# Row sums on one core: fifteen rows per partition in two buffers, in place of eight in five

## The chip, the cores and the metric

One core of a Trainium2 chip runs the kernel. The metric is the device time of one execution in microseconds (us); the time of a kernel is the median of its runs. The engines that matter here are VectorE (DVE in the profile), ScalarE (ACT), SyncE (SP), which issues the loads, and the core's 16 DMA engines, which carry them. A queue of an engine, written SPq or ACTq, holds its DMA issues in program order.

## What is computed

```python
def setup_inputs():
    batch, seq, dim = 32, 512, 1024
    return {
        "x": np.random.randn(batch, seq, dim).astype(np.float32),
        "divisor": float(dim),
    }

def reference(x, divisor):
    return (np.sum(x, axis=-1) / divisor).astype(np.float32)
```

The input is 16,384 rows of 1024 floats, 4 KiB a row and 67.1 MB in all. The output is one float per row, 64 KB.

## The kernel before

The rows are spread over the 128 partitions of the on-chip memory, 128 rows to a partition. What is loaded is summed along its rows by two engines side by side: DVE reduces several rows of a piece with one instruction (`reduce_sum`, L58), and ACT sums one row per instruction by copying it into a scratch tile `junk` with a running sum (`act_sum`, L53; the profile shows it as an ACTIVATE and a read of the accumulator). The function `sums` divides a piece: the last `for_act` rows go to ACT, the others to DVE.

The bulk is 15 tiles (the loop over `g`). A tile is 1024 consecutive rows, a block of 4 MiB, in which partition p has the 8 rows from 8p on, a contiguous run of 32 KiB (`xr`). Each tile is one load on SP's queue (L64) into one of five buffers (`bufs=5`); DVE takes 5 of its rows and ACT 3. A load into a buffer waits on SP until both engines have read what was there before. After the 7th and the 15th tile DVE multiplies the sums so far by 1/divisor (L68), and ACT's queue issues their store (L69), in runs of 8 floats.

The last 1024 rows, `xt`, are again 8 rows per partition. They come in pieces that get smaller, each with memory of its own: 4, 2 and 1 rows (`tail`, loaded at L73, half of each piece, rounded up, to ACT), and the last row in a half and two quarters (`last`, L81). DVE sums the half (L82), ACT the first quarter, then DVE multiplies the 7 finished tail sums by 1/divisor (L84), sums the last quarter (L85), adds the three parts (L86) and multiplies (L87), and SP stores the 8 results of each partition (L88).

Every engine runs its instructions in program order. So the store L69 stands on ACT's queue ahead of the tail's sums, and the tail's loads stand on SP's queue behind the bulk's. The waits between engines are put in by the tile framework, from which tile each instruction reads and writes.

Of the kernel before, what the change touches and what calls it, by code (L numbers as in the profile page):

```python
# [1 line left out]

# [4 lines left out]

F32 = mybir.dt.float32
ADD = mybir.AluOpType.add
MULT = mybir.AluOpType.mult  # L10
COPY = mybir.ActivationFunctionType.Copy
AX = mybir.AxisListType.X


@with_exitstack
def kernel(
    ctx: ExitStack,
    tc: tile.TileContext,
    x: bass.AP,
    divisor: float,  # L20
    out: bass.AP,
):
    nc = tc.nc
    xf = x.flatten_outer_dims()
    N, D = xf.shape
    P = nc.NUM_PARTITIONS
    scale = 1.0 / float(divisor)
    J = N // P
    assert J * P == N

    R, T = 8, 8
    G = (J - T) // R
    assert G * R + T == J
    n0 = G * P * R
    xr = bass.AP(tensor=x.tensor, offset=0, ap=[[R * D, P], [P * R * D, G], [D, R], [1, D]])
    xt = bass.AP(tensor=x.tensor, offset=n0 * D, ap=[[T * D, P], [D, T], [1, D]])
    ob = bass.AP(tensor=out.tensor, offset=0, ap=[[R, P], [P * R, G], [1, R]])
    ot = bass.AP(tensor=out.tensor, offset=n0, ap=[[T, P], [1, T]])  # L40
    tail = [4, 2, 1]
    pool = ctx.enter_context(tc.tile_pool(name="bulk", bufs=5))
    one = ctx.enter_context(tc.tile_pool(name="one", bufs=1))
    psum = ctx.enter_context(tc.tile_pool(name="junk", bufs=1, space=bass.MemoryType.PSUM))

    res = one.tile([P, G, R], F32, name="res")
    rest = one.tile([P, T], F32, name="rest")
    part = one.tile([P, 4], F32, name="part")
    junk = psum.tile([P, D], F32, name="junk")

    def act_sum(dst, src):
        n = src.shape[-1]
        nc.scalar.activation(junk[:, :n], src, COPY, accum_out=dst)  # L53

    def sums(t, o, rows, for_act):
        d = rows - for_act
        if d:
            nc.vector.reduce_sum(out=o[:, :d], in_=t[:, :d, :], axis=AX)  # L58
        for r in range(d, rows):
            act_sum(o[:, r : r + 1], t[:, r, :])  # L60

    for g in range(G):
        t = pool.tile([P, R, D], F32, name="t")
        nc.sync.dma_start(out=t, in_=xr[:, g])  # L64
        sums(t, res[:, g], R, 3)
        if g in (G // 2 - 1, G - 1):
            a = 0 if g < G - 1 else G // 2
            nc.vector.tensor_scalar_mul(out=res[:, a : g + 1], in0=res[:, a : g + 1], scalar1=scale)  # L68
            nc.scalar.dma_start(out=ob[:, a : g + 1], in_=res[:, a : g + 1])  # L69
    j = 0  # L70
    for k, rows in enumerate(tail):
        t = one.tile([P, rows, D], F32, name=f"tail{k}")
        nc.sync.dma_start(out=t, in_=xt[:, j : j + rows, :])  # L73
        sums(t, rest[:, j : j + rows], rows, (rows + 1) // 2)
        j += rows


    h, q = D // 2, D // 4
    last = one.tile([P, D], F32, name="last")
    for a, b in ((0, h), (h, h + q), (h + q, D)):  # L80
        nc.sync.dma_start(out=last[:, a:b], in_=xt[:, j, a:b])  # L81
    nc.vector.reduce_sum(out=part[:, 0:1], in_=last[:, 0:h], axis=AX)  # L82
    act_sum(part[:, 1:2], last[:, h : h + q])
    nc.vector.tensor_scalar_mul(out=rest[:, :j], in0=rest[:, :j], scalar1=scale)  # L84
    nc.vector.reduce_sum(out=part[:, 2:3], in_=last[:, h + q : D], axis=AX)  # L85
    nc.vector.reduce_sum(out=part[:, 3:4], in_=part[:, 0:3], axis=AX)  # L86
    nc.vector.tensor_scalar_mul(out=rest[:, j : j + 1], in0=part[:, 3:4], scalar1=scale)  # L87
    nc.sync.dma_start(out=ot, in_=rest)  # L88


# [1 line left out]
_INS = ['x', 'divisor']  # L92
_OUTS = [((32, 512), 'float32')]

_NUMBERS = {'divisor': 1024.0}


# [26 lines left out]
```

## Time and profile before

| what | value |
|---|---|
| median of 3 runs | 165.42 us (165.16 to 165.44) |
| profiled execution, its own time | 165.44 us |
| its span, first to last instruction | 163.7 us |
| DVE busy | 87.5 us (53%) |
| ACT busy | 58.1 us (35%) |
| DVE idle, waiting for a bulk load | 72.3 us |
| ACT idle, waiting for a bulk load | 98.4 us |
| DMA queue q1, the loads, share of 16 engines | 95.8% |
| DMA queue q10, small packets | 1952 packets, 0.06 MB, 0.7% |
| median time from issue to landing, a bulk load of 4 MiB | 43.0 us |

Times in the trace count from the start of the span. A landing is the moment at which an engine that waited for a load is let go. The time from issue to landing has the loads queued ahead in it: five may be under way.

### The profile page before, as it was taken

Reading aid. Unit: us, or ns where it says so; the run is one execution under the profiler, and the core shown is the slowest. Engines: PE = TensorE matmul, PEld = TensorE weight load, DVE = VectorE, ACT = ScalarE, POOL = GpSimd, SP = SyncE. Lnnn points to the kernel's source line nnn. Section 1 sums busy time; section 2 is a strip of 40 time slices with the busy share of each in tenths; the row PEclk is TensorE's granted clock in tenths of the full one; section 3 lists DMA queues with packets and bytes.
Section 4 is the critical chain, followed back from the end, with each engine's and each line's share of the span. In section 5 each row is a group of like instructions: output and inputs, shape, how many; then the busy total and the mean of one; then the engine's idle time right before and its main releaser. Section 6 shows DMA issues by size and latency. Waiting matters only on the chain.

```text
span 163.7 us, 226 instructions
## 1 busy us (share of the span) xinstructions
DVE 87.5 (53%) x24; ACT 58.1 (35%) x101; POOL 0.2 (0%) x4
## 2 busy tenths in 40 slices
DVE  0008548092763909367291843909357291854991
ACT  3008043070613508052260803508052260804393
POOL 0000000000000000000000000000000000000000
DMA  7899999998999999989999999999999999998980
GB/s 256 384 424 473 392 481 408 408 489 384 440 456 392 481 408 408 489 384 424 473 393 457 433 395 481 401 417 481 393 425 465 401 449 433 401 481 372 416 268 1
DMA packets 5121, 67.18 MB, mean 410 GB/s; under 512 B 2432, under 2 KB 2688, under 8 KB 2944
## 3 DMA queue, kind: packets, MB, share of 16 engines
q1 hardware_dynamic: 3168, 67.11, 95.8%
q10 hardware_dynamic: 1952, 0.06, 0.7%
q14 instruction: 1, 0.01, 0.0%
HBM read 67.11 MB, written 0.07 MB: 410 GB/s over the span
## 4 chain that ended last, share of the span: by engine, by line
DMA 83%; DVE 11%; issue 2%; ACT 1%; SPq 1%; ACTq 0%; DVEq 0%
DMA t<-in_x_dram 83%; DVE res L58 10%; ACT junk L53 1%; SPq L64 1%; ACTq L69 0%; DVE part L85 0%; DVE res L68 0%; DVE rest L84 0%; DVE part L86 0%; DVE rest L87 0%; DVEq L86 0%; DVEq L68 0%
## 5 line engine op out<-in xcount | busy, mean ns | idle before, releaser
L58 DVE TENSOR_REDUCE res<-t 128x5 f32<-128x5120 f32 x15 | 82.3, 5488 | 72.3 <-DMA t<-in_x_dram 72.3
L53 ACT ACTIVATE junk<-t 128x1024 f32<-128x1024 f32 x45 | 46.2, 1027 | 99.3 <-DMA t<-in_x_dram 98.4
L53 ACT ACTIVATION_READ_ACCUMULATOR junk<-t 128x1 f32 x45 | 8.4, 186 | 0.0
L53 ACT ACTIVATE junk<-tail 128x1024 f32<-128x1024 f32 x4 | 4.1, 1027 | 2.8 <-DVE res L68 2.7
L58 DVE TENSOR_REDUCE rest<-tail 128x2 f32<-128x2048 f32 (+1 forms) x2 | 3.4, 1745 | 0.0
L53 ACT ACT_TABLE_LOAD x1 | 1.3, 1283 | 0.7 <-PEq L105 0.7
L82 DVE TENSOR_REDUCE part<-last 128x1 f32<-128x512 f32 x1 | 0.7, 686 | 0.2 <-DMA last<-in_x_dram 0.2
L53 ACT ACTIVATION_READ_ACCUMULATOR junk<-tail 128x1 f32 x4 | 0.7, 186 | 0.0
L84 DVE TENSOR_SCALAR rest<-rest 128x7 f32<-128x7 f32 x1 | 0.2, 170 | 0.9 <-ACT junk L53 0.9
L68 DVE TENSOR_SCALAR res<-res 128x56 f32<-128x56 f32 (+1 forms) x2 | 0.4, 193 | 0.2
L85 DVE TENSOR_REDUCE part<-last 128x1 f32<-128x256 f32 x1 | 0.4, 410 | 0.0
L53 ACT ACTIVATE junk<-last 128x256 f32<-128x256 f32 x1 | 0.4, 387 | 0.0
L86 DVE TENSOR_REDUCE part<-part 128x1 f32<-128x3 f32 x1 | 0.2, 156 | 0.1
L53 ACT ACTIVATION_READ_ACCUMULATOR junk<-last 128x1 f32 x1 | 0.2, 186 | 0.0
L87 DVE TENSOR_SCALAR rest<-part 128x1 f32<-128x1 f32 x1 | 0.2, 156 | 0.0
L105 POOL MEMSET const-bfloat16-1.0<- 128x1 bf16 x1 | 0.1, 102 | 0.0
L105 POOL MEMSET const-uint8-127<- 128x1 uint8 x1 | 0.1, 102 | 0.0
L105 POOL MEMSET const-float32-1.0<- 128x1 f32 x1 | 0.1, 99 | 0.0
L105 POOL MEMSET const-float32-0.0<- 128x1 f32 x1 | 0.1, 98 | 0.2 <-issue 0.2
## 6 DMA issues: line engine op xcount, KB each, us to landing
t<-in_x_dram SPq DMA_DIRECT2D x15, 4096.0 KB, 43.0
tail<-in_x_dram SPq DMA_DIRECT2D x1, 2048.0 KB, 11.0
tail<-in_x_dram SPq DMA_DIRECT2D x1, 1024.0 KB, 13.1
tail<-in_x_dram SPq DMA_DIRECT2D x1, 512.0 KB, 13.9
last<-in_x_dram SPq DMA_DIRECT2D x1, 256.0 KB, 14.1
last<-in_x_dram SPq DMA_DIRECT2D x2, 128.0 KB, 13.9
out_dram<-res ACTq DMA_DIRECT2D x1, 32.0 KB, 4.9
out_dram<-res ACTq DMA_DIRECT2D x1, 28.0 KB, 66.4
```

The costliest lines, as they stand in the source:

```text
L53: nc.scalar.activation(junk[:, :n], src, COPY, accum_out=dst)
L58: nc.vector.reduce_sum(out=o[:, :d], in_=t[:, :d, :], axis=AX)
L64: nc.sync.dma_start(out=t, in_=xr[:, g])
L68: nc.vector.tensor_scalar_mul(out=res[:, a : g + 1], in0=res[:, a : g + 1], scalar1=scale)
L82: nc.vector.reduce_sum(out=part[:, 0:1], in_=last[:, 0:h], axis=AX)
L84: nc.vector.tensor_scalar_mul(out=rest[:, :j], in0=rest[:, :j], scalar1=scale)
L85: nc.vector.reduce_sum(out=part[:, 2:3], in_=last[:, h + q : D], axis=AX)
L86: nc.vector.reduce_sum(out=part[:, 3:4], in_=part[:, 0:3], axis=AX)
L87: nc.vector.tensor_scalar_mul(out=rest[:, j : j + 1], in0=part[:, 3:4], scalar1=scale)
L105: nc = _bacc.Bacc("TRN2", target_bir_lowering=False, num_devices=1)
```

## The change

The rows are dealt out in another way: partition p now owns the 128 consecutive rows from 128p on, so that its share of the input is one contiguous run of 512 KiB, and its share of the output one run of 512 B. The bulk is 8 loads of 15 rows per partition (a run of 60 KiB in each) into two buffers; DVE takes 8 rows of a load and ACT 7. The tail has the same pieces as before (4, 2 and 1 rows, and a row in a half and two quarters), now from the end of each partition's own run. All sums go to one tile `res` of 128 columns. The multiplies and stores inside the bulk loop are gone: one multiply takes the first 127 columns at the end, and one store from SP writes everything.

```diff
-    R, T = 8, 8
-    G = (J - T) // R
-    assert G * R + T == J
-    n0 = G * P * R
-    xr = bass.AP(tensor=x.tensor, offset=0, ap=[[R * D, P], [P * R * D, G], [D, R], [1, D]])
-    xt = bass.AP(tensor=x.tensor, offset=n0 * D, ap=[[T * D, P], [D, T], [1, D]])
-    ob = bass.AP(tensor=out.tensor, offset=0, ap=[[R, P], [P * R, G], [1, R]])
-    ot = bass.AP(tensor=out.tensor, offset=n0, ap=[[T, P], [1, T]])
+    xr = x.tensor.reshape((P, J, D)).ap()
+    out_v = out.tensor.reshape((P, J)).ap()
+    bulk = [15] * 8
     tail = [4, 2, 1]
-    pool = ctx.enter_context(tc.tile_pool(name="bulk", bufs=5))
+    assert sum(bulk) + sum(tail) + 1 == J
+    pool = ctx.enter_context(tc.tile_pool(name="bulk", bufs=2))
...
-    res = one.tile([P, G, R], F32, name="res")
-    rest = one.tile([P, T], F32, name="rest")
+    res = one.tile([P, J], F32, name="res")
...
-    def sums(t, o, rows, for_act):
+    def sums(t, j, rows, for_act):
         d = rows - for_act
         if d:
-            nc.vector.reduce_sum(out=o[:, :d], in_=t[:, :d, :], axis=AX)
+            nc.vector.reduce_sum(out=res[:, j : j + d], in_=t[:, :d, :], axis=AX)
         for r in range(d, rows):
-            act_sum(o[:, r : r + 1], t[:, r, :])
+            act_sum(res[:, j + r : j + r + 1], t[:, r, :])
 
-    for g in range(G):
-        t = pool.tile([P, R, D], F32, name="t")
-        nc.sync.dma_start(out=t, in_=xr[:, g])
-        sums(t, res[:, g], R, 3)
-        if g in (G // 2 - 1, G - 1):
-            a = 0 if g < G - 1 else G // 2
-            nc.vector.tensor_scalar_mul(out=res[:, a : g + 1], in0=res[:, a : g + 1], scalar1=scale)
-            nc.scalar.dma_start(out=ob[:, a : g + 1], in_=res[:, a : g + 1])
     j = 0
+    for rows in bulk:
+        t = pool.tile([P, 15, D], F32, name="t")
+        nc.sync.dma_start(out=t[:, :rows, :], in_=xr[:, j : j + rows, :])
+        sums(t, j, rows, rows * 7 // 15)
+        j += rows
     for k, rows in enumerate(tail):
         t = one.tile([P, rows, D], F32, name=f"tail{k}")
-        nc.sync.dma_start(out=t, in_=xt[:, j : j + rows, :])
-        sums(t, rest[:, j : j + rows], rows, (rows + 1) // 2)
+        nc.sync.dma_start(out=t, in_=xr[:, j : j + rows, :])
+        sums(t, j, rows, (rows + 1) // 2)
         j += rows
...
-        nc.sync.dma_start(out=last[:, a:b], in_=xt[:, j, a:b])
+        nc.sync.dma_start(out=last[:, a:b], in_=xr[:, j, a:b])
...
-    nc.vector.tensor_scalar_mul(out=rest[:, :j], in0=rest[:, :j], scalar1=scale)
+    nc.vector.tensor_scalar_mul(out=res[:, :j], in0=res[:, :j], scalar1=scale)
...
-    nc.vector.tensor_scalar_mul(out=rest[:, j : j + 1], in0=part[:, 3:4], scalar1=scale)
-    nc.sync.dma_start(out=ot, in_=rest)
+    nc.vector.tensor_scalar_mul(out=res[:, j : j + 1], in0=part[:, 3:4], scalar1=scale)
+    nc.sync.dma_start(out=out_v, in_=res)
```

## The prediction

> **What bounds the kernel now.** I read the chain that ended last first, because it says which resource the end hangs on, and the memory line beside it.
>
> ```profile
> HBM read 67.11 MB, written 0.07 MB: 410 GB/s over the span
> ...
> DMA 83%; DVE 11%; issue 2%; ACT 1%; SPq 1%; ACTq 0%; DVEq 0%
> ```
>
> The span is a read stream of 67 MB, with little around it. So two things have a price: the pace of the stream, and what is left once the stream has delivered its last large piece. For the pace I cut the span at the landings of the bulk loads (columns: stretch, its length, DVE, ACT and POOL busy, clock, DMA share, GB/s).
>
> ```profile
> 22.60:32.30 9.70, 5.49 (x1) 3.45 (x6) 0.00 (x0) 1.00 1.00 432
> ...
> 90.70:100.90 10.20, 5.46 (x2) 3.45 (x6) 0.00 (x0) 1.00 1.02 435
> ```
>
> All 16 DMA engines are busy all the time, and DVE and ACT are half idle. The timeline has DVE starting on the second load at 22.62 and on the eighth at 80.89 us: (80.89 - 22.62) / 6 = 9.712 us per load of 8 rows per partition, 1.214 us a row. One interval took 10.22 us, and the DMA view of that window shows what only it has, one packet of instructions:
>
> ```profile
> q1 hardware_dynamic: 151, 4.42, 99.7%
> q10 hardware_dynamic: 151, 0.00, 0.8%
> q14 instruction: 1, 0.01, 0.2%
> ```
>
> While q10, the small packets of the first result store, runs (its DMA is on its way from 77.0 to 143.4 us), the other intervals are hardly longer: 110.61 to 139.77 is 3 x 9.720.
>
> Then the end, in the timeline (start, length, engine and line):
>
> ```profile
> 149.47 5.49 DVE L58 TENSOR_REDUCE res<-t 128x5 f32<-128x5120 f32 x1 [4.21 <-DMA t<-in_x_dram]
> ...
> 155.29 0.38 ACTq L69 DMA_DIRECT2D out_dram<-res  x1
> 155.72 1.03 ACT L53 ACTIVATE junk<-tail 128x1024 f32<-128x1024 f32 x1 [2.68 <-DVE res L68]
> ...
> 156.90 1.03 ACT L53 ACTIVATE junk<-tail 128x1024 f32<-128x1024 f32 x1
> ...
> 159.26 1.03 ACT L53 ACTIVATE junk<-tail 128x1024 f32<-128x1024 f32 x1
> 160.22 0.19 ACT L53 ACTIVATION_READ_ACCUMULATOR junk<-tail 128x1 f32 x1
> 160.44 0.39 ACT L53 ACTIVATE junk<-last 128x256 f32<-128x256 f32 x1
> 160.44 0.17 DVE L84 TENSOR_SCALAR rest<-rest 128x7 f32<-128x7 f32 x1 [0.94 <-ACT junk L53]
> ...
> 161.22 0.16 DVE L87 TENSOR_SCALAR rest<-part 128x1 f32<-128x1 f32 x1
> 161.44 0.35 SPq L88 DMA_DIRECT2D out_dram<-rest  x1
> ```
>
> Call T the landing of the last bulk load, 149.44 in the chain. The last arithmetic ends at 161.38 = T + 11.94, and ACT sets it: it is through with its 3 bulk rows at 153.04, stands 2.68 us behind the store L69 in its own queue (which waits for DVE's multiply L68), does four tail rows at 1.18 us each, and L84 on DVE waits 0.94 us for the last. The data had come earlier: the last pieces were issued from 144.7 to 145.7 and took 13.8 to 14.1 us, so all was in by about 159.5.
>
> **Part 1, the stream up to T.** Before, 15 loads of 8 rows come ahead of T; after, 8 loads of 15 rows: 120 rows both times, and 8 rows behind T both times. At 1.214 us a row T does not move: the first load lands 7 x 1.214 = 8.5 us later, at 21.43, and seven more take 7 x 18.21 = 127.5, together 148.93, plus the 0.50 of the long interval, 149.43. Three small terms:
> - Packets. In a window of 5 us q1 moved 2.10 MB in 80 packets, 16 of them under 512 B: 64 of 32 KiB, a load's whole run in a partition. A run of 15 rows is 60 KiB. If it too is one packet, each engine has 64 of them instead of 120, 56 fewer. A packet's cost of its own: q10's 1952 took 0.7% of 16 x 163.7 us, 9.4 ns each, at most; at least what they added to the stream, 9.720 - 9.712 = 8 ns per interval for about 8 packets per engine, 1 ns each. So the gain is 0.06 to 0.53 us. I take 0.06, since the 1 ns was measured in the stream itself.
> - The first store's small packets go: 7 intervals x 0.008 and the 0.06 by which the interval from 80.89 to 90.66 was long make 0.1 us.
> - The instruction packet. I keep its 0.50. ACT's instructions go from 101 to 1 + 2 x 61 = 123, DVE's from 24 to 8 + 2 + 5 = 15; I can't see which engine's code it was. Bounds: none (-0.50) or two (+0.50).
>
> T comes at 149.44 - 0.06 - 0.10 = 149.28.
>
> The Trainium skill (DMA: Bandwidth & Descriptors, Why small descriptors are slow) gives about 3 cycles per packet. At 0.85 GHz my estimate from it is 56 x 3.5 ns = 0.2 us in place of 0.06.
>
> The stretch that no row shows is the order of addresses. Before, neighbouring partitions read 32 KiB apart in one block of 4 MiB; after, they read 512 KiB apart across the whole input. The rows bound it only widely: from the quickest interval seen (9.69, 0.2% less, -0.3 us) to the slowest (10.22 against 9.712, 5.2%, 145.7 x 0.052 = +7.6 us). I take nothing for it, because the tail, read from 128 places 32 KiB apart in runs of 16 down to 1 KiB, kept the bulk's pace: 2 MiB from 149.44 to 154.4 is 4.96 us for 4 x 1.214 = 4.86. I keep both ends.
>
> A rule speaks against the change here. The same page (Latency and other measured facts, the row on HBM row pitch) has copies between HBM tensors at 207 GB/s per direction with partitions 512 KiB apart, against 214 at full rate, and half of that at 4 MiB. Scaled to the stream that would be 145.7 x 0.034 = 4.9 us, an estimate from the page; no run here shows such a pitch yet.
>
> **Part 2, buffers and queues.** With two buffers, load g + 2 waits on SP until DVE is through with load g. The reduce is now of 8 rows. From the rows of 2048 elements (2279 ns) and 5120 (5487 ns) an element costs 1.044 ns, so 8192 take 8.70 us; ACT's 7 rows take 7 x 1.18 = 8.26. The refill goes out at 8.72 after a landing, plus 0.33 for the issue, plus at most the 2.49 us that the first load lost (12.20 to landing for 9.71 of data): data can flow at 11.5, and the load in flight lasts 18.2. Cost nothing, with 6.7 us of cover; were it gone, each microsecond of lateness would count six times, once per refill. Behind the waiting refill on SP stand the later loads, and behind the last one the six tail loads: they are issued near 21.43 + 5 x 18.21 + 8.72 = 121.2 us and the 3 us after, 25 us ahead of T. Before, they were held 36.6 us for the first store:
>
> ```profile
> SPq L73 <- DMA out_dram<-res: 36.6, 1, 36.6
> SPq L88 <- DVE rest L87: 15.3, 1, 15.3
> ```
>
> That wait goes, and is worth nothing: they went out at 143.4, six us ahead of T.
>
> **Part 3, from T to the end.** This is where I see the cost. The last bulk piece is 15 rows at once in place of 8. ACT starts at T + 0.09 and has 7 bulk rows and then 4 tail rows with no wait: each tail row is there long before (the last whole one 7 x 1.214 = 8.5 us after T; ACT comes to it at T + 11.9). Ten periods of 1.18 and 1.15 for the last make 12.95, so T + 13.04. Before, this point was 160.41 = T + 10.97. As a balance: four more bulk rows, +4.72, less the stall behind L69, -2.68. DVE comes a little earlier: 8.72, then 2 rows and 1 row of tail (2.28, 1.21) and half of the last row (0.69), each overlapped by 0.08, T + 12.7; it waits again for ACT at the multiply. From ACT's last sum to the last arithmetic it was 161.38 - 160.41 = 0.97; the multiply now has 127 columns, not 7 (170 ns at 7, 195 at 64: 0.44 ns each, +0.05). The end is T + 14.06 in place of T + 11.94: **+2.12 us**. The second store L69 and multiply L68 are gone with the stall; the one store left carries 64 KB in runs of 512 B, not 4 KB in runs of 32 B. At an engine's 27 GB/s (432 / 16) that is 8 x 18 ns more, 0.15 at most; I take +0.10.
>
> **The sum.** 149.28 + 14.06 = 163.34; from the last arithmetic to the end of the span 163.7 - 161.38 = 2.32, plus 0.10: a span of 165.76 in place of 163.7. The profiled execution took 165.44, 1.74 outside the span, and the median of the runs is 165.42. So **167.5 us**, +2.1 (1.2%).
>
> **Rivals.**
> - *The spread addresses slow the stream.* Place: every bulk interval, 18.21 us. Price from 0.5 to 7.6 us, in the middle 3.8: 171.3. For it: nothing in the trace has such a pitch. Against: the pace was the same for all runs from 32 to 1 KiB, and the DMA engines at 100% look like the limit. A 60 KiB run cut into 4 KiB packets belongs here: 840 more packets per engine at 1 to 9.4 ns are 0.8 to 7.9 us; the 8-row runs were not cut.
> - *The larger packets speed the stream* by more than the drain costs. Place: the same intervals, which would come under 17.95 us: the 2.1 us are 1.4% of 145.7, or 37 ns for each of the 56 packets, the point from which it decides. At 2% it gains 2.9 us: 164.6, faster than before. Against it: 1 ns measured, 9.4 as the bound, and no interval under 9.69.
> - *The refill starves.* If a load could not be queued beside the one in flight, six gaps of 2.49 us: 167.5 + 14.9 = 182.4. Against it: five loads were issued one after the other at the start, each 9.7 us behind the other in landing.
>
> **How the numbers follow.** Forecast 63%, slow stream 28%, quick stream 7%, starved 2%. The forecast's own range is 166.2 (no instruction packet -0.50, the full packet gain -0.47, the quickest interval -0.3) to 168.0 (a second instruction packet). Spread evenly, the 28% from +0.5 to +7.6 leave 10% above 172.6 and 12% above 172.1; with the 7% below that is near 2 in 10, so 166.2 to 172.1. What this kernel's measurement can tell from no change is about 0.2%, 0.33 us: faster has 6% and within it 1%, both from the quick stream, and slower 93%.
>
> **What would show it.** Intervals of 18.2 us between bulk landings and T near 149.3 bear out part 1; 18.5 or more is the slow stream, under 17.95 the quick one. DVE's reduce near 8.70, ACT without idle time after T, the multiply waiting for ACT, and 14.1 us from T to the last arithmetic bear out part 3. It is wrong if ACT or DVE waits for a tail piece, or if a gap in the DMA share follows a landing.

## The result, and the profile after

The changed kernel takes 167.39 us (median of 4 runs, 167.34 to 167.50), against 165.38 for the kernel before (4 runs): a ratio of 1.0125, 95% interval 1.0108 to 1.0143. That is 2.0 us slower; 167.5 was predicted. The profiled execution took 167.34 us with a span of 165.6.

The page of the changed kernel first, its memory line and its chain that ended last:

```profile
HBM read 67.11 MB, written 0.07 MB: 406 GB/s over the span
...
DMA 73%; DVE 16%; ACT 5%; issue 3%; SPq 0%; DVEq 0%; ACTq 0%
```

The share of DMA in the chain fell from 83% to 73%, and that of DVE and ACT together rose from 12% to 21%. That alone is no proof of a longer end: the chain follows a refill back through the reduce that released it, here and before. The stages tell more. The stream, cut at the landings (stretch, length, DVE, ACT and POOL busy, clock, DMA share, GB/s):

```profile
58.05:76.20 18.15, 8.69 (x1) 8.04 (x14) 0.00 (x0) 1.00 1.00 433
76.20:94.35 18.15, 8.69 (x1) 8.04 (x14) 0.00 (x0) 1.00 1.00 433
94.35:112.70 18.35, 8.69 (x1) 8.04 (x14) 0.00 (x0) 1.00 0.99 429
```

The DMA engines are still busy all the time, at 433 GB/s where it was 432. So the stream lost nothing. The last bulk piece lands where its part of the chain ends, shown here before and after:

```profile
106.43 43.02 DMA t<-in_x_dram
...
121.47 27.53 DMA t<-in_x_dram
```

That is T = 149.00, and before it was 149.44. Now the end, in the timeline of the changed kernel:

```profile
149.02 8.69 DVE L53 TENSOR_REDUCE res<-t 128x8 f32<-128x8192 f32 x1 [9.46 <-DMA t<-in_x_dram]
149.08 1.03 ACT L48 ACTIVATE junk<-t 128x1024 f32<-128x1024 f32 x1 [9.92 <-DMA t<-in_x_dram]
...
157.34 1.03 ACT L48 ACTIVATE junk<-tail 128x1024 f32<-128x1024 f32 x1
157.63 3.40 DVE L53 TENSOR_REDUCE res<-tail 128x2 f32<-128x2048 f32 x2
...
160.89 1.03 ACT L48 ACTIVATE junk<-tail 128x1024 f32<-128x1024 f32 x1
160.94 0.68 DVE L74 TENSOR_REDUCE part<-last 128x1 f32<-128x512 f32 x1
162.07 0.39 ACT L48 ACTIVATE junk<-last 128x256 f32<-128x256 f32 x1
162.07 0.23 DVE L76 TENSOR_SCALAR res<-res 128x127 f32<-128x127 f32 x1 [0.45 <-ACT junk L48]
...
162.92 0.15 DVE L79 TENSOR_SCALAR res<-part 128x1 f32<-128x1 f32 x1
163.13 0.35 SPq L80 DMA_DIRECT2D out_dram<-res  x1
```

After T neither engine waits for data any more: no brackets with a DMA stand behind the tail's lines. ACT goes through eleven rows one after the other, and DVE waits 0.45 us for the last of them. The arithmetic ends at 163.07, T + 14.07, where it was T + 11.94. The stream gave back 0.4 us, the end took 2.1, and the store with what closes the span took 0.2 more (2.53 us in place of 2.32).

### The profile page after: what moved, and what is told of

Same layout as the page of the kernel before. It is cut to its first block, busy times and chain, and to the rows that moved or that the text cites. A ratio compares the mean times of both kernels' runs of the same rounds, so it can differ in the third digit from the quotient of the medians.

```text
span 165.6 us, 219 instructions
## 1 busy us (share of the span) xinstructions
DVE 74.3 (45%) x15; ACT 70.7 (43%) x123; POOL 0.2 (0%) x4
## 4 chain that ended last, share of the span: by engine, by line
DMA 73%; DVE 16%; ACT 5%; issue 3%; SPq 0%; DVEq 0%; ACTq 0%
DMA t<-in_x_dram 73%; DVE res L53 16%; ACT junk L48 5%; SPq L60 0%; DVE part L77 0%; DVE res L76 0%; DVE part L78 0%; DVE res L79 0%; DVEq L78 0%; ACTq L48 0%
## 5 line engine op out<-in xcount | busy, mean ns | idle before, releaser
L53 DVE TENSOR_REDUCE res<-t 128x8 f32<-128x8192 f32 x8 | 69.5, 8686 | 88.2 <-DMA t<-in_x_dram 88.2
L48 ACT ACTIVATE junk<-t 128x1024 f32<-128x1024 f32 x56 | 57.5, 1027 | 91.0 <-DMA t<-in_x_dram 89.5
L48 ACT ACTIVATION_READ_ACCUMULATOR junk<-t 128x1 f32 x56 | 10.4, 186 | 0.0
L53 DVE TENSOR_REDUCE res<-tail 128x2 f32<-128x2048 f32 (+1 forms) x2 | 3.4, 1743 | 0.0
```

The costliest lines, as they stand in the source:

```text
L53: nc.vector.reduce_sum(out=res[:, j : j + d], in_=t[:, :d, :], axis=AX)
```

## The experiments

Times are medians; each is compared with runs of the kernel before on the same chip, 165.2 to 165.3 us.

**A smaller last piece.**

```diff
-    bulk = [15] * 8
-    tail = [4, 2, 1]
+    bulk = [15] * 7 + [8]
+    tail = [7, 4, 2, 1]
...
-        sums(t, j, rows, (rows + 1) // 2)
+        sums(t, j, rows, (rows + 1) // 2 if rows < 7 else 3)
```

> The eighth bulk load is cut into 8 rows in the second buffer and 7 rows in memory of their own, so that 7 rows and not 15 land last. Theory (what is left to sum after the last large landing sets the end, on ACT): ACT has 3 rows after T, until T + 3.6, then follows the data: the last whole row lands 7 x 1.21 = 8.5 us after T, its sum ends at T + 9.7, the arithmetic at T + 10.7 in place of 14.03. With T at 149.0 as in the changed kernel: 164.0 us. Rival (the stream or the store sets the end): no change, 167.4.

Measured: 164.36 us, ratio to before 0.9948 (0.9935 to 0.9961), 3.0 us under the changed kernel. Its timeline after the 7 rows landed:

```profile
149.20 4.42 DVE L53 TENSOR_REDUCE res<-tail 128x4 f32<-128x4096 f32 x1 [3.03 <-DMA tail<-in_x_dram]
...
154.14 1.03 ACT L48 ACTIVATE junk<-tail 128x1024 f32<-128x1024 f32 x1 [1.37 <-DMA tail<-in_x_dram]
...
156.63 1.03 ACT L48 ACTIVATE junk<-tail 128x1024 f32<-128x1024 f32 x1 [0.17 <-DMA tail<-in_x_dram]
157.93 1.03 ACT L48 ACTIVATE junk<-tail 128x1024 f32<-128x1024 f32 x1
...
160.00 0.15 DVE L79 TENSOR_SCALAR res<-part 128x1 f32<-128x1 f32 x1
```

ACT now waits for the data of the tail (1.37, 0.17), and the end is 160.15, 10.97 us after the landing at 149.18. The landing is within 0.2 us of T in the changed kernel. (ACT also has six of these 15 rows and not seven; the last experiment shows that this alone gains nothing.) So the cost was the size of the last large piece, and the stream and the buffers had no part in it.

**The same piece, but through the two buffers.**

```diff
-    bulk = [15] * 8
+    bulk = [15] * 7 + [8, 7]
```

> The same cut, but the 7 rows go into the first buffer, which is free only when DVE is through with the seventh load. Theory (a refill needs 2.9 us from issue to landing beyond its data, so two buffers have cover only while the load in flight is long): the 7-row load is issued 8.7 us after the seventh landing, the 8-row load in flight lasts 9.7, so the stream stands still for 8.7 + 2.9 - 9.7 = 1.9 us, and the tail after it: 165.9 us. Rival (a refill needs no head start): as with memory of its own, 164.0.

Measured: 166.34 us, ratio 1.0064 (1.0050 to 1.0079). In its timeline the landing of the 7 rows comes 10.8 us after that of the 8, though they are 8.5 us of data:

```profile
130.76 8.69 DVE L53 TENSOR_REDUCE res<-t 128x8 f32<-128x8192 f32 x1 [9.45 <-DMA t<-in_x_dram]
...
140.47 5.49 DVE L53 TENSOR_REDUCE res<-t 128x5 f32<-128x5120 f32 x1 [1.02 <-DMA t<-in_x_dram]
...
151.28 4.42 DVE L53 TENSOR_REDUCE res<-t 128x4 f32<-128x4096 f32 x1 [5.33 <-DMA t<-in_x_dram]
```

The 2.0 us to the kernel with memory of its own are the hole in the stream. Two buffers have cover in the changed kernel because a 15-row load is 18 us long; beside a 9.7 us load it is gone. From the release, 130.76 + 8.69, to the landing at 151.28 are 11.83 us, 3.4 more than the 8.47 of its data.

**The old stall behind the store.** In the kernel before:

```diff
-            nc.scalar.dma_start(out=ob[:, a : g + 1], in_=res[:, a : g + 1])
+            if g < G - 1:
+                nc.scalar.dma_start(out=ob[:, a : g + 1], in_=res[:, a : g + 1])
...
+    nc.sync.dma_start(out=ob[:, G // 2 : G], in_=res[:, G // 2 : G])
     nc.vector.reduce_sum(out=part[:, 0:1], in_=last[:, 0:h], axis=AX)
```

> The kernel before, with the second store issued from SP behind the tail's loads, not from ACT. Theory (the store's wait in ACT's queue was part of the old end): ACT begins the tail when its first piece lands and follows the data, last whole row in at about 158.2, summed at 159.4 and not 160.4: 1.0 us less, 164.4. Rival (the old end hung on the data or on DVE): 165.4.

Measured: 164.22 us, ratio 0.9941 (0.9928 to 0.9953). In its timeline:

```profile
154.34 1.03 ACT L53 ACTIVATE junk<-tail 128x1024 f32<-128x1024 f32 x1 [1.40 <-DMA tail<-in_x_dram]
...
155.19 0.40 SPq L83 DMA_DIRECT2D out_dram<-res  x1
```

ACT starts the tail at 154.34, when it lands, and not at 155.72 behind the store. The end comes 1.0 us sooner. So moving the store was a gain that the change had in it, and the larger piece hid it.

**A late refill.**

```diff
-        sums(t, j, rows, rows * 7 // 15)
+        sums(t, j, rows, 7 if j == 105 else 0)
```

> The changed kernel with DVE alone summing the 15 rows of the first seven loads (16.2 us by 1.044 ns an element), so that each refill is released 16.2 us after a landing and ready 2.9 us later, 0.95 us past the 18.15 of the load in flight. Theory now (lateness counts once for each pair of loads, since the late load gives the next refill more time): 3 x 0.95 = 2.9 us, 170.2. As the prediction said it (six times): 5.7 us, 173.1. Rival (a refill needs no head start): 167.4. If the one instruction packet was ACT's, it goes, with the 0.2 us of its interval.

Measured: 176.29 us (four runs from 175.33 to 177.69, the trace is of the slowest), ratio 1.0673 (1.0630 to 1.0716). No theory had the size. The timeline shows the pattern:

```profile
40.07 16.15 DVE L53 TENSOR_REDUCE res<-t 128x15 f32<-128x15360 f32 x1 [1.99 <-DMA t<-in_x_dram]
61.53 16.16 DVE L53 TENSOR_REDUCE res<-t 128x15 f32<-128x15360 f32 x1 [5.30 <-DMA t<-in_x_dram]
79.66 16.15 DVE L53 TENSOR_REDUCE res<-t 128x15 f32<-128x15360 f32 x1 [1.98 <-DMA t<-in_x_dram]
```

Every second interval is long, 21.46 and then 18.13: lateness counts three times and not six, as expected. But each time it is 3.3 to 3.6 us and not 0.95. The refill released at 38.07 landed at 61.5, 23.4 us later, 5.3 more than the 18.15 of its data; the first load of the changed kernel had 2.9. So this refill cost more than a load at the start. That it found the DMA engines nearly empty doesn't explain it alone: the refill of the second experiment found them empty too, and cost 3.4. The transfer rate in slices of 0.1 us (a packet of 60 KiB in one slice reads 614) shows where part of it lies: at the start of the changed kernel the first packets of the 16 engines come within 1.2 us, here from 39.0 us on within 2.5:

```profile
GB/s 614 1229 1843 614 614 614 0 614 0 0 0 0 0 0 0 614 0 614 614 0 614 0 0 614 614 0 0 0 0 0 0 1229 0 1229 614 614 614 0 614 614
```

By the packets' own records in the two traces these first packets are longer as well: 3.1 to 3.8 us here, 2.7 to 3.3 at the start, 2.27 in the stream. The last of them ends 7.2 us after the release here, and 4.8 us after the issue at the start; the 2.4 us between are the whole difference of 5.3 to 2.9. What spreads and slows them is open. This kernel also has no instruction packet, with 25 ACT instructions in place of 123, so the one in the other traces was most likely code for ACT.

**Addresses close together.**

```diff
-    xr = x.tensor.reshape((P, J, D)).ap()
+    xb = bass.AP(tensor=x.tensor, offset=0, ap=[[15 * D, P], [P * 15 * D, 8], [D, 15], [1, D]])
+    xt = bass.AP(tensor=x.tensor, offset=120 * P * D, ap=[[8 * D, P], [D, 8], [1, D]])
...
-        nc.sync.dma_start(out=t[:, :rows, :], in_=xr[:, j : j + rows, :])
+        nc.sync.dma_start(out=t[:, :rows, :], in_=xb[:, j // 15])
```

(and the tail's loads from `xt`)

> The changed kernel with its loads of 15 rows taken from contiguous blocks (partitions 60 KiB apart, the tail 32 KiB apart), as the kernel before took its 8; the sums land in the same places of the tile, so the output is in another order than the reference's. Theory (the spread of addresses costs nothing): 18.15 us per load, first landing near 21.8, 167.4 us. Rival (the spread costs something that the larger packets hide): shorter intervals, by what it costs; 1% would be 0.18 us a load and 1.5 us in all, 165.9. If the first landing comes back to 21.4, its 0.35 us were the spread's.

Measured: 167.14 us, ratio 1.0115 (1.0099 to 1.0131), which overlaps that of the changed kernel. In its timeline DVE starts on loads at 58.04 and 76.20, with the first at 21.75:

```profile
58.04 8.69 DVE L54 TENSOR_REDUCE res<-t 128x8 f32<-128x8192 f32 x1 [9.46 <-DMA t<-in_x_dram]
76.20 8.69 DVE L54 TENSOR_REDUCE res<-t 128x8 f32<-128x8192 f32 x1 [9.48 <-DMA t<-in_x_dram]
```

18.16 us, as with the rows spread. The spread of addresses costs nothing, and the late first landing isn't its doing.

**Addresses spread, runs of 8 rows.**

```diff
-    bulk = [15] * 8
+    bulk = [8] * 15
-    pool = ctx.enter_context(tc.tile_pool(name="bulk", bufs=2))
+    pool = ctx.enter_context(tc.tile_pool(name="bulk", bufs=5))
...
-        t = pool.tile([P, 15, D], F32, name="t")
+        t = pool.tile([P, 8, D], F32, name="t")
```

> The changed kernel with 15 loads of 8 rows in five buffers, partitions still 512 KiB apart: runs of 32 KiB. Theory (9 ns per packet, nothing for the spread): 9.71 us per load as before, first landing 12.93; no store in ACT's way, so the arithmetic ends about 10.7 to 10.8 us after T at 149.2, 164.2 us. Rival (the quicker rows come from the order of addresses, not from the packets): 8 x 1.2098 = 9.68 us per load, T near 148.7, 163.7. Rival (the spread slows runs of 32 KiB): over 9.8 us per load.

Measured: 164.76 us, ratio 0.9970 (0.9958 to 0.9981), 0.6 over what was expected. The undisturbed intervals are 9.71 to 9.72:

```profile
120.48 5.49 DVE L53 TENSOR_REDUCE res<-t 128x5 f32<-128x5120 f32 x1 [4.23 <-DMA t<-in_x_dram]
130.20 5.49 DVE L53 TENSOR_REDUCE res<-t 128x5 f32<-128x5120 f32 x1 [4.22 <-DMA t<-in_x_dram]
139.91 5.49 DVE L53 TENSOR_REDUCE res<-t 128x5 f32<-128x5120 f32 x1 [4.22 <-DMA t<-in_x_dram]
```

So runs of 32 KiB go at their old pace with partitions 512 KiB apart, and the quicker rows of the changed kernel come from its larger packets. Of the 0.6 us, 0.47 lie in a first landing at 13.40 (12.93 before) and most of the rest in the end, 10.96 us after T where 10.7 to 10.8 was expected. Single intervals are up to 9.83; the average over all 14, (149.62 - 13.40) / 14 = 9.730, is that of the kernel with the store from SP, (149.37 - 13.12) / 14 = 9.732.

**Packets of 12 KiB.**

```diff
-        nc.sync.dma_start(out=t[:, :rows, :], in_=xr[:, j : j + rows, :])
+        for i in range(0, rows, 3):
+            nc.sync.dma_start(out=t[:, i : i + 3, :], in_=xr[:, j + i : j + i + 3, :])
```

> The changed kernel with each bulk load issued as five loads of 3 rows per partition into the same buffer: runs of 12 KiB, 40 packets per engine and buffer in place of 8. Theory now (9 ns for each packet of a load): 32 x 9 = 0.29 us more for 15 rows, 18.44 us; the last landing at 151.3. As the prediction took it (1 ns): 18.18, the last landing at 149.3. In both the engines begin on a buffer before its last part lands, so only 3 of ACT's 7 rows are left after the last landing and the arithmetic ends 10.7 us after it: 166.3 us by the theory, 164.3 by 1 ns.

Measured: 166.63 us, ratio 1.0075 (1.0062 to 1.0088). The starts of DVE, each on the first parts of a buffer:

```profile
14.41 8.69 DVE L53 TENSOR_REDUCE res<-t 128x8 f32<-128x8192 f32 x1 [14.41 <-DMA t<-in_x_dram]
32.85 8.69 DVE L53 TENSOR_REDUCE res<-t 128x8 f32<-128x8192 f32 x1 [9.76 <-DMA t<-in_x_dram]
51.30 8.69 DVE L53 TENSOR_REDUCE res<-t 128x8 f32<-128x8192 f32 x1 [9.76 <-DMA t<-in_x_dram]
```

18.44 and 18.45 us per buffer; six of the seven intervals average 18.445, and the one with the instruction packet took 18.96. That is 0.30 over the 18.147 of whole loads, for 32 packets of data more on each engine and four small ones, since each load ends with one: 8.3 ns each.

**Another division of the last piece.**

```diff
-        sums(t, j, rows, rows * 7 // 15)
+        sums(t, j, rows, 6 if j == 105 else 7)
```

> The changed kernel with the last bulk load split 9 rows to DVE and 6 to ACT, in place of 8 and 7. Theory (ACT sets the end by 0.4 us over DVE, and both are near full after T): DVE gets 1.04 us more and is through with its half row at T + 13.7, which then sets the end: about T + 14.65, 0.6 us more, 168.0. Rival (ACT alone is too full, a better split would undo the cost): up to 1.2 us less, 166.2.

Measured: 167.81 us, ratio 1.0155 (1.0141 to 1.0169), 0.4 over the changed kernel. In its timeline:

```profile
148.97 9.75 DVE L53 TENSOR_REDUCE res<-t 128x9 f32<-128x9216 f32 x1 [9.46 <-DMA t<-in_x_dram]
...
160.84 0.39 ACT L48 ACTIVATE junk<-last 128x256 f32<-128x256 f32 x1
161.96 0.67 DVE L74 TENSOR_REDUCE part<-last 128x1 f32<-128x512 f32 x1
```

ACT is done with its whole rows 1.2 us before DVE has come to its last half row, and DVE's end, 163.54, is T + 14.6. Both engines are full after T; a row moved from one to the other only changes which of them is last. The cost is how much is left, not how it is shared.

## Why the prediction was right

**The end, T + 14.06: right**, 14.07 measured. The reduce of 8 rows took 8.69 us (8.70), ACT's eleven rows ran without a wait, the multiply of 127 columns took 227 ns, and DVE waited for ACT. The first experiment takes this term away with three microseconds of time and leaves T in place; the eighth shows that the division isn't what fails. The two parts of its balance have been shown apart: the store behind which ACT stood was worth 1.0 us in the kernel before by itself (third experiment). The -2.68 of the prediction is the length of the stall, and stood in a balance with four more rows; by itself the stall was worth less, since the tail's first piece came 1.4 us into it. For the same reason the four rows cost 3.1 us by themselves (from T + 10.97 in the first and third experiments to T + 14.07), and not 4.72: with three rows ACT waits for the tail's data. Both terms were too large by about 1.6 us, and their difference was right.

**T at 149.28: right within 0.28 us**, with four terms off that nearly cancel; that it came so close is luck. The larger packets gained more than the 0.06 that was taken: 7 x (18.21 - 18.147) = 0.44 us by the intervals alone. From 9.712 us for eight runs of 32 KiB per engine and 18.147 for eight of 60 KiB, the bytes go at 27.19 GB/s, and 0.071 us of a load go beside its bytes. A load gives each engine eight packets of data and a small one at its end, as the window of one load (76.2 to 94.3 us) has it:

```profile
DMA packets 144, 7.86 MB, mean 434 GB/s; under 512 B 16, under 2 KB 16, under 8 KB 16
```

So that is 7.9 ns for each of nine packets. All bulk loads here have this shape, and the intervals alone could as well be a cost per load; the packets' own records (the traces hold each packet with its start and length) say that it is one per packet: 1213 ns for 32 KiB, 2267 for 60 KiB, 46 for 1 KiB and 9 for the four bytes at the end (medians), each 7 to 9 ns over its bytes at that rate. This is near the far bound, 9.4, from the busy time of the small packets; the bound I chose, from what the small packets of a store added to the stream, was the wrong one for the loads' own packets. The Trainium skill's 3 cycles per packet (DMA: Bandwidth & Descriptors, Why small descriptors are slow), 3.5 ns by my estimate, are also too few for these loads. The instruction packet's interval was 0.21 us late and not 0.50. The 0.10 for the first store's small packets should not have been taken off: the sum of 149.43 goes by the pace of the intervals up to that store, so it had no such cost in it. Against the packets and the instruction packet, the first load landed at 21.78 and not 21.43: its start cost 2.90 us and not 2.49. Part of this may be scatter, since the first load of 8 rows landed at 12.93, 13.12 and 13.40 in three traces.

**The spread of addresses, taken at nothing: right**, by the fifth and sixth experiments. The rule on the HBM row pitch (same page, Latency and other measured facts) would have had 4.9 us here; it was measured on copies within HBM, and loads at this pitch ran at 433 GB/s.

**The buffers, taken at nothing: right in the result, too generous in the working.** No refill of the changed kernel is late, but the start of a refill cost 3.4 us in the second experiment and 5.3 to 5.7 in the fourth, not the 0.33 + 2.49 assumed. With 5.7 the cover is 18.15 - 8.72 - 5.7 = 3.7 us and not 6.7. That a late refill counts six times was wrong: a late load gives the next refill the time it needs, and it counted three times.

**The last store and the close** took 2.53 us, 0.11 more than the 2.42 of the sum.

## What to carry to other kernels

When a stream is at the pace of the DMA engines, look at what is left to compute when its last large piece lands: the four rows more that ACT had to sum after the last landing cost 3.1 us of end here, while the larger packets gave back 0.4 us in all. Make the last pieces small, and give them memory of their own, because a two-buffer ring has cover only while the load in flight is longer than the compute on the other buffer and the start of a refill together. And keep a store that waits for one engine out of the queue of another that still has sums to do: that alone made the old kernel 1.0 us quicker, 164.22, the best time measured here, close to the 164.36 of the changed kernel with a small last piece.

## What was not expected of the hardware

A packet of a load costs 8 ns beside its bytes (7.9 from loads of 32 against 60 KiB runs, 8.3 from 12 against 60 KiB), while the small packets of the store beside the stream added about 1 ns each to the load intervals, though each took 9 ns by its own record. A refill of 60 KiB runs landed 5.3 us later than its data takes, against 2.9 at the start of the kernel: the first packets of the 16 engines were spread over 2.5 us in place of 1.2, and took up to 3.8 us. A refill of 28 KiB runs behind a load of 8 rows cost only 3.4, and why the other costs more stays open. The one instruction packet cost its interval anything from nothing (with addresses close together) to 0.5 us (the kernel before).
